# Layer B of a decoder trunk: splitting the next product's first weight piece inside the current product

## The chip, the core and the metric

The kernel runs on one core of a Trainium2 chip. The metric is the device time of one execution in microseconds, the median of several runs. The core's engines are named here as the profile names them: PE (TensorE, matmuls; PEld is its weight loads), DVE (VectorE), ACT (ScalarE), POOL (GpSimd) and SP (SyncE, which issues the DMAs of this kernel). TensorE's operands come from SBUF, and its sums go to PSUM.

## The reference, cut to what matters

A decoder trunk of two layers on 256 tokens of width 2048. Layer A is a Mamba-2 mixer. From its output come the keys and values that layer B, a dilated window attention with three head groups, uses. What layer B computes with large weights:

```python
k, v = jnp.split(x @ kv_w, 2, axis=-1)                 # kv_w: 2048 x 6144
shift, scale, gate = _adaln(c, ada_w[1], ada_b[1])     # silu(c) @ w + b, three columns of 2048
h = x * (1.0 + scale) + shift
q, z = jnp.split(h @ in_w, [DIL_Q_WIDTH], axis=-1)     # in_w: 2048 x 4096
o = ...                                                # attention of q over k, v, three groups merged
y = (o * jax.nn.silu(z)) @ out_w
x = _layer_norm(DEEPNORM_ALPHA * x + (1.0 + gate) * y, ln_g[1], ln_b[1])
```

All arrays are float32.

## The kernel before, in words

**Precision by splitting.** A float32 product is made of fp32r matmuls. Each operand is cut into a high half (a rounded copy) and a low half (the rest), and high x high, high x low and low x high are added up in PSUM. For weights this is `split` (L96): ScalarE copies `raw` to `whi` (L99), VectorE subtracts to `wlo` (L101). The activations of layer B stand ready split, as `xhi` and `xlo`, side by side in `xp`.

**Pieces and products.** Weights come in pieces of 128x1024 numbers, 512 KB each. `load_piece` (L91) has SP issue the DMA of one (L93) into one of six `raw` buffers; `whi` and `wlo` have four buffers each. A product runs over all 2048 rows of a weight block. `cm_wide` (L139) makes a block of 256 columns from four pieces; for each piece it runs eight matmuls of `whi` with both halves of the activations (L149, 512 columns) and eight of `wlo` with the high half (L152, 256 columns), in turns of two. `tm_chunk` (L181) makes a block of 512 columns from eight pieces (L173 to L175). The sums of a product take two of the four accumulators of the pool `mm`, so two products can be in PSUM at a time. Then they are emptied: after `cm_wide` by a copy on ScalarE (L156) and an addition on VectorE (L157) for each of two accumulators, after the value products by two copies on ScalarE in `evict_v` (L799).

**Layer B in order.** The value products of the first half (`wv`, the third of them by `tm_chunk`, L852), twelve key products by `cm_wide` (`wk`, L857), three more value products by `tm_chunk` (L859), the adaLN step on `xhi` and `xlo` (L863 to L868), six query products (`queries(0)`, L892 to L897), attention of the first four heads, six more query products, attention of the other four heads, four products of the gate path (`z_gate`), then the output product and the LayerNorm.

**The background.** `queue` (L267) makes a list of jobs, and `background` (L106) takes jobs from it at the end of each piece, at a rate that the product is given. In the key and value products the rate is one job for every two pieces. A job is a step of adaLN: it has SP load the next 128x2048 block of `ada_w` into one of two `araw` buffers (L244, 1 MB), and VectorE multiplies the block loaded before with silu(c) and adds up the products (L251). In the query products there is one job for every piece, sixteen in all (`weigh`, L878): products and sums on VectorE (L886), with two loads of rows (L63) in every fourth.

**What sets the order.** The program is traced once, and a planner sets the order of instructions on each engine: it plays the program through with its own costs, and gives an engine that is free the earliest traced of the instructions that are ready then. On the chip each engine, and SP's queue as well, runs its list in this fixed order and waits where it must. So the order on an engine is near the order of the trace, but an instruction that was ready later in the planner's play stands later. `tc.issue_after(ins)` queues what a block traces on the engine of `ins` behind `ins`; it orders the queue and does not wait for `ins` to end. The lists `copied` and `latest` hold the instructions of L99 and L101 as they are traced.

The order of the trace at the end of a product is now: load and split of the last piece, its matmuls, a background job if one is due, the two evictions, load and split of the next product's first piece, its matmuls.

Of the kernel before, what the change touches and what calls it, by code (L numbers as in the profile page):

```python
# [12 lines left out]
AF = mybir.ActivationFunctionType  # L13
ALU = mybir.AluOpType
# [7 lines left out]
KT = D // P  # L22
# [5 lines left out]
NG = 3  # L28
# [21 lines left out]
def trunk(ctx, tc, xT, x, c, par, cst, bias, lnrow, ada, wdt, win, wxs, wout, wk, wv, wbin, wbout, out):  # L50
    nc = tc.nc
    V, S, T, PO = nc.vector, nc.scalar, nc.tensor, nc.gpsimd
# [38 lines left out]
    def load_piece(src):  # L91
        raw = wp.tile([P, 1024], F32, name="raw", bufs=6)
        nc.sync.dma_start(raw, src)  # L93
        return raw

    def split(raw, into=None, after=None):  # L96

        hi, lo = into or [wp.tile([P, 1024], F32R, name=n, bufs=4) for n in ("whi", "wlo")]
        copied.append(S.activation(hi, raw, AF.Copy))  # L99
        with tc.issue_after(after) if after is not None else ExitStack():  # L100
            latest.append(V.tensor_tensor(lo, raw, hi.bitcast(F32), op=ALU.subtract))  # L101
        return hi.rearrange("p (k n) -> p k n", k=2), lo.rearrange("p (k n) -> p k n", k=2)

    jobs, latest, copied, pin = [], [], [], [None]

    def background(n, every=1):  # L106

# [7 lines left out]
    def cm_piece(src, q, ps, ahi, alo, k0=0, k1=KT, w=None, after=None):  # L115


        hi, lo = w or split(load_piece(src[q]), after=after)
        for k in range(2):
            kt = 2 * q + k  # L120
            for n in range(4):
                o = ps[n // 2][:, n % 2, :]
                c_ = slice(n * P, n * P + P)
                first = kt == k0 and n % 2 == 0
                T.matmul(o, hi[:, k, c_], ahi[:, kt, :], start=first, stop=False, skip_group_check=True)  # L125
                T.matmul(o, hi[:, k, c_], alo[:, kt, :], start=False, stop=False, skip_group_check=True)  # L126
                T.matmul(o, lo[:, k, c_], ahi[:, kt, :], start=False, stop=kt == k1 - 1, skip_group_check=True)  # L127
# [4 lines left out]
    def cm_quad(src, ahi, alo, rate=(0, 1), k0=0):  # L132
        ps = acc_pair()
        for q in range(k0 // 2, KT // 2):
            cm_piece(src, q, ps, ahi, alo, k0=k0)
            background(*rate)
        return ps

    def cm_wide(src, dst, rate=(0, 1), moving=None):  # L139

        both, high = moving or (lambda kt: xp[:, kt], lambda kt: xhi[:, kt, :])
        ps = acc_pair()
        for q in range(KT // 4):
            hi, lo = (t.rearrange("p k n -> p (k n)").rearrange("p (k n) -> p k n", k=4)
                      for t in split(load_piece(src[q])))
            for k in range(4):
                kt = 4 * q + k
                for n in range(2):
                    T.matmul(ps[n], hi[:, k, n * P:n * P + P], both(kt), start=kt == 0, stop=False,  # L149
                             skip_group_check=True)  # L150
                for n in range(2):
                    T.matmul(ps[n][:, 0, :], lo[:, k, n * P:n * P + P], high(kt), start=False, stop=kt == KT - 1,  # L152
                             skip_group_check=True)
            background(*rate)
        for n in range(2):
            S.activation(dst[:, n, :], ps[n][:, 1, :], AF.Copy)  # L156
            V.tensor_tensor(dst[:, n, :], ps[n][:, 0, :], dst[:, n, :], op=ALU.add)  # L157

    def tiles(ps):
        return [ps[n // 2][:, n % 2, :] for n in range(4)]  # L160
# [1 line left out]
    def tm_piece(src, q, ps, ahi, alo, k0=0, k1=KT, w=None):  # L162

        tm_mults(q, w or split(load_piece(src[q])), ps, ahi, alo, k0, k1, range(2))
# [16 lines left out]
    def tm_chunk(src, ahi, alo, nk=KT, rate=(0, 1), k0=0, pre=None, split_end=0):  # L181

        ps = tm_pair()
        n = nk // 2 - split_end
        for q in range(k0 // 2, n):
            if pre:
                pre(q)
            tm_piece(src, q, ps, ahi, alo, k0, nk)
            background(*rate)
        held = [(q, split(load_piece(src[q]))) for q in range(n, nk // 2)]  # L190
        for b in range(2):
            for q, w in held:
                tm_mults(q, w, ps, ahi, alo, k0, nk, (b,))
        return ps
# [63 lines left out]
    def gate_out(layer):  # L258

        ada_bias(layer, slice(0, KT), slice(2, 3))  # L260
        pt = aux.tile([P, 512], F32, name="aux")[:KT, :P]
        T.transpose(pt, mod[layer][:, :, 2], ident)
        row = sm.tile([KT, P], F32, name="row", bufs=1)
        V.tensor_copy(row, pt)
        nc.sync.dma_start(gated[layer].rearrange("(k p) -> k p", p=P), row)
# [24 lines left out]
    with ExitStack() as cA:  # L290
# [14 lines left out]
        with ExitStack() as cS:  # L305
# [75 lines left out]
            with ExitStack() as c0:  # L381
# [42 lines left out]
                for row in ("b4:0. b6:0. h z2:0. b2:0 x1:0 h", "b2:1. x1:1. z1:0 z1:1. z4:0 h h",  # L424
# [3 lines left out]
                    for w in row.split():  # L428
                        if w == two:
                            n = -2 if sum(o[0] == -2 for o in order) == sum(o[0] == -1 for o in order) else -1  # L430
# [359 lines left out]
    kv, vt = {}, {}  # L790
# [4 lines left out]

    def evict_v(hq, g, ps):
        vt[hq, g] = place(3 * hq + g if hq == 0 else 9 + g, [P, 2, 512])
        for b in range(2):
            S.activation(vt[hq, g][:, b, :], ps[b], AF.Copy)  # L799

    with ExitStack() as cL:
        pl = cL.enter_context(tc.tile_pool(name="pl", bufs=3))

        vps = [tm_pair(), tm_pair()]
        def high(i, b):
            for k in range(2):
                kt = 2 * (i // 2) + k
                for w in first_v[i]:
                    T.matmul(vps[i % 2][b], hx(kt)[:, b * P:b * P + P], w[:, k, :], start=kt == 0 and w is first_v[i][0],  # L809
                             stop=False)  # L810

        def low(i, b):
            for k in range(2):
                T.matmul(vps[i % 2][b], lx(2 * (i // 2) + k)[:, b * P:b * P + P], first_v[i][0][:, k, :], start=False,
                         stop=False)

        end, _ = x_quad(0)
        with tc.issue_after(end.ins):
            for n in range(1, 4):
                normalise(0, 512 * n, 512 * n + 512)  # L820
        for i in range(4):
            high(i, 0)
        for i in range(4):
            if i == 2:
                _, tile4 = x_quad(1)
                for n in range(1, 4):
                    normalise(1, 512 * n, 512 * n + 512)
            low(i, 0)
        for i in range(4):
            high(i, 1)  # L830
            if i == 2:
                x_tile(4)
                x_tile(5)
        for i in range(4):
            low(i, 1)
        for q in range(2, KT // 2):
            if q < KT // 2 - 1:
                x_tile(2 * q + 2)
                x_tile(2 * q + 3)
            for j in range(2):  # L840
                w = split(load_piece(wv[2 * j][q]), after=tile4.ins if q == 2 else None)
                tm_mults(q, w, vps[j], hx, lx, 0, KT, range(2))
        for g in range(2):
            evict_v(0, g, vps[g])

        R = (1, 2)
        pin[0] = latest[-1].ins
        with tc.issue_after(tile4.ins):
            state[0] = 0
            queue(pl, cols1[11:])  # L850
            jobs.append(lambda: gate_out(1))
            evict_v(0, 2, tm_chunk(wv[4], hx, lx, rate=R))  # L852
            for hq in range(2):
                for g in range(NG):
                    kv[hq, g] = place(3 + 3 * hq + g, [P, 4, L])
                    for w in range(2):
                        cm_wide(wk[2 * (2 * g + hq) + w], kv[hq, g][:, 2 * w:2 * w + 2, :], rate=R)  # L857
            for g in range(NG):
                evict_v(1, g, tm_chunk(wv[1 + 2 * g], hx, lx, rate=R))  # L859
            drain()  # L860
            late = latest[-1].ins

        ada_bias(1, slice(0, KT), slice(0, 2))  # L863
        for kt in range(KT):
            t = pl.tile([P, L], F32, name="htmp")
            S.activation(t, xhi[:, kt, :].bitcast(F32), AF.Identity, bias=shift(1, kt), scale=scale(1, kt))
            V.scalar_tensor_tensor(t, xlo[:, kt, :].bitcast(F32), scale(1, kt), t, op0=ALU.mult, op1=ALU.add)
            split_act(xhi[:, kt, :], xlo[:, kt, :], t)  # L868
# [22 lines left out]

    def queries(hq):  # L892
        qq = [pc2.tile([P, 4, L], F32, name=f"q{g}") for g in range(NG)]
        for g in range(NG):
            for w in range(2):
                cm_wide(wbin[2 * (2 * g + hq) + w], qq[g][:, 2 * w:2 * w + 2, :], rate=(1, 1))
        return qq  # L897
# [107 lines left out]
    ps = [tm_pair() for _ in range(2)]  # L1005
# [140 lines left out]
```

## Time and profile before

| | us |
|---|---|
| time, median of 3 runs | 1253.88 |
| lowest and highest of the runs | 1252.72, 1255.48 |
| the profiled execution's own time | 1253.52 |
| its span, first to last instruction | 1251.7 |
| PE busy | 1218.4 |
| weight loads of PE busy | 1043.1 |
| DVE busy | 1031.0 |
| ACT busy | 704.5 |

Everything that the profile shows belongs to the one profiled execution. A row of a timeline has the start in microseconds from the span's start, the duration (of all merged instructions), engine, line of the source, operation, what is written from what is read, the number of instructions merged (x2), and in brackets the idle time of the engine ahead of it and what ended that idle time. A row of the waits has who waited for whom: microseconds in total, times, the longest. A row of the busy time by stretch has the stretch, its length, busy time and number of instructions of PE, PEld, DVE, ACT and POOL, the granted clock of TensorE, the share of time that the DMA engines were busy, and GB/s. The ends of matmuls are modelled by the profiler.

The key, value and query products of layer B lie between about 750 and 1130 us of the span; the granted clock is 1.00 there.

### The profile page before, as it was taken

The numbers are of one execution on the slowest core, as the hardware profiler recorded it, in microseconds if no ns is written. First come the engines' busy times: TensorE is split into PE (matmuls) and PEld (weight loads), VectorE is DVE, ScalarE is ACT, GpSimd is POOL, SyncE is SP. The second block draws the span as 40 slices with busy tenths as digits, with TensorE's granted clock in tenths as the row PEclk, the third lists the DMA queues.
The fourth block names the chain that finished last, engine by engine and source line by source line (L and its number), as shares of the span: only waits on it lengthen the run. The fifth ranks groups of instructions, "written<-read, shape, count | busy, mean of one in ns | idle before, by whom it ended". The sixth has DMA issues, their size and how long they took to land.

```text
span 1251.7 us, 18740 instructions
## 1 busy us (share of the span) xinstructions
PE 1218.4 (97%) x7086; PEld 1043.1 (83%) x7086; DVE 1031.0 (82%) x1454; ACT 704.5 (56%) x1045; POOL 0.2 (0%) x4
## 2 busy tenths in 40 slices
PE   4999999999999999999999999999999999999997
PEld 4889998898888878788888788888878888888886
DVE  6999986999987988899778678879888866758777
ACT  3655477869588788754444544434445644445631
POOL 0000000000000000000000000000000000000000
PEclk9999999999999999999999999999999999999999
DMA  9999977687657556699998569989998774464641
GB/s 381 422 421 423 420 253 257 207 286 285 203 179 219 170 155 198 220 321 342 354 313 305 183 199 377 364 318 348 359 381 317 242 241 142 126 207 122 228 176 67
DMA packets 80586, 335.88 MB, mean 268 GB/s; under 512 B 9104, under 2 KB 9328, under 8 KB 67696
## 3 DMA queue, kind: packets, MB, share of 16 engines
q1 hardware_dynamic: 80496, 334.69, 74.7%
q8 instruction: 55, 0.90, 0.3%
q14 instruction: 35, 0.29, 0.1%
HBM read 332.47 MB, written 2.18 MB: 267 GB/s over the span
## 4 chain that ended last, share of the span: by engine, by line
PE 86%; DVE 6%; DMA 5%; issue 1%; ACT 1%; SPq 0%; DVEq 0%; ACTq 0%
PE acc L149 20%; PE acc L174 12%; PE acc L175 12%; PE acc L173 12%; PE acc L152 10%; PE acc L125 4%; PE acc L127 3%; PE acc L126 3%; DMA raw<-in_wk 3%; DMA araw<-in_ada 2%; DVE araw L251 1%; DVE wlo L101 1%; PE py L625 1%; DMA raw<-in_wv 1%; PE acc L809 1%
## 5 line engine op out<-in xcount | busy, mean ns | idle before, releaser
L99 ACT ACTIVATE whi<-raw 128x1024 fp32r<-128x1024 f32 x392 | 412.3, 1058 | 383.1 <-PE acc L175 142.1
L101 DVE TENSOR_TENSOR wlo<-raw,whi 128x1024 fp32r<-128x1024 f32 x392 | 473.5, 1222 | 141.0 <-ACT whi L99 137.0
L149 PE MATMUL acc<-actT,whi 128*128 128x512 f32 x1280 | 406.3, 398 | 0.0
L152 PEld LDWEIGHTS acc<-actT,wlo 128*128 128x128 f32 x1280 | 239.7, 188 | 62.2 <-DVE wlo L101 7.2
L174 PE MATMUL acc<-wlo,actT 128*128 128x512 f32 x688 | 269.9, 392 | 0.6 <-DVE wlo L101 0.5
L173 PE MATMUL acc<-whi,actT 128*128 128x512 f32 x688 | 266.6, 394 | 1.2 <-ACT actT L681 1.2
L152 PE MATMUL acc<-actT,wlo 128*128 128x256 f32 x1280 | 254.1, 280 | 3.9 <-DVE wlo L101 3.8
L251 DVE SCALAR_TENSOR_TENSOR araw<-araw,cb__72 128x2048 f32<-128x2048 f32 x96 | 219.4, 2285 | 8.9 <-DMA araw<-in_ada 8.6
L149 PEld LDWEIGHTS acc<-actT,whi 128*128 128x128 f32 x1280 | 196.5, 189 | 0.4
L175 PE MATMUL acc<-whi,actT 128*128 128x512 f32 x432 | 168.8, 391 | 0.0
L174 PEld LDWEIGHTS acc<-wlo,actT 128*128 128x128 f32 x688 | 129.3, 188 | 28.5 <-DVE wlo L101 2.8
L173 PEld LDWEIGHTS acc<-whi,actT 128*128 128x128 f32 x688 | 128.8, 188 | 27.2 <-ACT actT L681 1.7
L125 PE MATMUL acc<-actT,whi 128*128 128x256 f32 x384 | 109.0, 288 | 17.5 <-ACT actT L414 17.3
L126 PE MATMUL acc<-actT,whi 128*128 128x256 f32 x384 | 108.8, 286 | 0.0
L127 PE MATMUL acc<-actT,wlo 128*128 128x256 f32 x384 | 106.7, 286 | 1.9 <-DVE wlo L101 1.9
L175 PE MATMUL acc<-whi,ylo 128*128 128x512 f32 x256 | 100.7, 394 | 0.0
L175 PEld LDWEIGHTS acc<-whi,actT 128*128 128x128 f32 x432 | 81.1, 188 | 16.7
L125 PEld LDWEIGHTS acc<-actT,whi 128*128 128x128 f32 x384 | 74.3, 194 | 18.9 <-ACT actT L414 17.5
L127 PEld LDWEIGHTS acc<-actT,wlo 128*128 128x128 f32 x384 | 73.4, 195 | 2.2 <-DVE wlo L101 2.1
L126 PEld LDWEIGHTS acc<-actT,whi 128*128 128x128 f32 x384 | 74.7, 194 | 0.3
L175 PEld LDWEIGHTS acc<-whi,ylo 128*128 128x128 f32 x256 | 48.1, 188 | 9.7
L583 ACT ACTIVATE seg<-cbc,cumT 128x128 f32<-128x128 f32 x128 | 41.2, 390 | 5.6 <-PE py L625 4.9
(262 smaller groups left out, 1054.3 us busy)
## 6 DMA issues: line engine op xcount, KB each, us to landing
araw<-in_ada SPq DMA_DIRECT2D x96, 1024.0 KB, 7.7
raw<-in_win SPq DMA_DIRECT2D x112, 512.0 KB, 6.5
raw<-in_wout SPq DMA_DIRECT2D x64, 512.0 KB, 5.7
raw<-in_wbin SPq DMA_DIRECT2D x64, 512.0 KB, 4.1
raw<-in_wxs SPq DMA_DIRECT2D x48, 512.0 KB, 4.6
raw<-in_wv SPq DMA_DIRECT2D x48, 512.0 KB, 6.0
raw<-in_wk SPq DMA_DIRECT2D x48, 512.0 KB, 8.3
cbc<-cumd SPq DMA_DIRECT2D x16, 512.0 KB, 4.8
```

What stands on the lines that cost most here:

```text
L99: copied.append(S.activation(hi, raw, AF.Copy))
L101: latest.append(V.tensor_tensor(lo, raw, hi.bitcast(F32), op=ALU.subtract))
L125: T.matmul(o, hi[:, k, c_], ahi[:, kt, :], start=first, stop=False, skip_group_check=True)
L126: T.matmul(o, hi[:, k, c_], alo[:, kt, :], start=False, stop=False, skip_group_check=True)
L127: T.matmul(o, lo[:, k, c_], ahi[:, kt, :], start=False, stop=kt == k1 - 1, skip_group_check=True)
L149: T.matmul(ps[n], hi[:, k, n * P:n * P + P], both(kt), start=kt == 0, stop=False, skip_group_check=True)
L152: T.matmul(ps[n][:, 0, :], lo[:, k, n * P:n * P + P], high(kt), start=False, stop=kt == KT - 1, skip_group_check=True)
L173: T.matmul(o, h_, hi[:, k, :], start=kt == k0, stop=False, skip_group_check=part)
L174: T.matmul(o, h_, lo[:, k, :], start=False, stop=False, skip_group_check=part)
L175: end = T.matmul(o, l_, hi[:, k, :], start=False, stop=kt == k1 - 1, skip_group_check=part)
L251: V.scalar_tensor_tensor(raw, raw, 1.0, cb_, op0=ALU.mult, op1=ALU.mult, accum_out=mod[layer][:, ct, j:j + 1])
L583: S.activation(seg[:, hh, b, :], cbc[:, hh, b, :], AF.Relu, bias=cumT[:, b, h0 + hh:h0 + hh + 1], scale=-1.0)
```

## The change

The list `upcoming` names the products whose first piece is to be split early. When a product has split its own last piece and not yet traced its matmuls, `begin_next` loads and splits piece 0 of the next product in the list and keeps it in `ready`; the next product takes it from there (`first_or`). While `ready` holds a piece, `behind_next` queues the evictions on ScalarE behind the copy of that piece (`copied[-1]`) and those on VectorE behind its subtraction (`latest[-1]`).

The list is filled at two places. Ahead of the third value product: the twelve key products and the three value products that follow. In `queries`: the last five of its six query products. Elsewhere the list is empty, and then the order of the trace is as before. In a product that has a successor in the list, the order of the trace becomes: load and split of the last piece, load and split of the next product's first piece, the last piece's matmuls, a background job if one is due, the two evictions.

```diff
     jobs, latest, copied, pin = [], [], [], [None]
+    upcoming, ready = [], []
+
+    def first_or(src, q):
+
+        return ready.pop() if ready else split(load_piece(src[q]))
+
+    def begin_next():
+
+        if upcoming:
+            src, q = upcoming.pop(0)
+            ready.append(split(load_piece(src[q])))
+
+    def behind_next():
+
+        stack = ExitStack()
+        if ready:
+            stack.enter_context(tc.issue_after(copied[-1].ins))
+            stack.enter_context(tc.issue_after(latest[-1].ins))
+        return stack
...
     def cm_wide(src, dst, rate=(0, 1), moving=None):
...
         for q in range(KT // 4):
-            hi, lo = (t.rearrange("p k n -> p (k n)").rearrange("p (k n) -> p k n", k=4)
-                      for t in split(load_piece(src[q])))
+            w = first_or(src, q)
+            if q == KT // 4 - 1:
+                begin_next()
+            hi, lo = (t.rearrange("p k n -> p (k n)").rearrange("p (k n) -> p k n", k=4) for t in w)
...
-        for n in range(2):
-            S.activation(dst[:, n, :], ps[n][:, 1, :], AF.Copy)
-            V.tensor_tensor(dst[:, n, :], ps[n][:, 0, :], dst[:, n, :], op=ALU.add)
+        with behind_next():
+            for n in range(2):
+                S.activation(dst[:, n, :], ps[n][:, 1, :], AF.Copy)
+                V.tensor_tensor(dst[:, n, :], ps[n][:, 0, :], dst[:, n, :], op=ALU.add)
...
     def tm_chunk(src, ahi, alo, nk=KT, rate=(0, 1), k0=0, pre=None, split_end=0):
...
-            tm_piece(src, q, ps, ahi, alo, k0, nk)
+            w = first_or(src, q)
+            if q == nk // 2 - 1:
+                begin_next()
+            tm_piece(src, q, ps, ahi, alo, k0, nk, w=w)
...
     def evict_v(hq, g, ps):
...
-        for b in range(2):
-            S.activation(vt[hq, g][:, b, :], ps[b], AF.Copy)
+        with behind_next():
+            for b in range(2):
+                S.activation(vt[hq, g][:, b, :], ps[b], AF.Copy)
...
+            upcoming.extend((wk[2 * (2 * g + hq) + w], 0) for hq in range(2) for g in range(NG) for w in range(2))
+            upcoming.extend((wv[1 + 2 * g], 0) for g in range(NG))
             evict_v(0, 2, tm_chunk(wv[4], hx, lx, rate=R))
...
     def queries(hq):
         qq = [pc2.tile([P, 4, L], F32, name=f"q{g}") for g in range(NG)]
+        upcoming.extend([(wbin[2 * (2 * g + hq) + w], 0) for g in range(NG) for w in range(2)][1:])
```

`cm_quad`, which makes products of layer A, is changed in the same way as `tm_chunk`; the list is empty there.

More of the change, by code (lines that the diff above doesn't have):

```diff
@@ L134, in cm_quad @@
         for q in range(k0 // 2, KT // 2):
-            cm_piece(src, q, ps, ahi, alo, k0=k0)
+            w = first_or(src, q)
+            if q == KT // 2 - 1:
+                begin_next()
+            cm_piece(src, q, ps, ahi, alo, k0=k0, w=w)
             background(*rate)
@@ L187, in tm_chunk @@
                 pre(q)
-            tm_piece(src, q, ps, ahi, alo, k0, nk)
+            w = first_or(src, q)
+            if q == nk // 2 - 1:
+                begin_next()
+            tm_piece(src, q, ps, ahi, alo, k0, nk, w=w)
             background(*rate)
```

## The prediction

> **What bounds the kernel now.** I read the busy shares of the page first.
>
> ```profile
> span 1251.7 us, 18740 instructions
> ...
> PE 1218.4 (97%) x7086; PEld 1043.1 (83%) x7086; DVE 1031.0 (82%) x1454; ACT 704.5 (56%) x1045; POOL 0.2 (0%) x4
> ```
>
> TensorE is busy for 1218.4 of 1251.7 us. All its idle time is 33 us, and only the part that lies in layer B behind a product boundary can be what this change is after. The second view is the list of waits: a row of PE for the whole run, then rows for the stretch 840 to 960 us.
>
> ```profile
> PE acc L152 <- DVE wlo L101: 3.8, 7, 2.1
> ```
> ```profile
> PEld acc L152 <- DVE wlo L101: 4.3, 6, 1.4
> ...
> PEld acc L174 <- DVE wlo L101: 1.7, 4, 0.5
> PE acc L152 <- DVE wlo L101: 1.5, 5, 0.9
> ```
>
> In layer B, TensorE waits only for `wlo`, the low half of a weight piece, which VectorE makes (L101); it never waits for `whi`, nor for an accumulator. Because the ends of matmuls are modelled, I take the loss from boundaries and not from these gaps. The third view is busy time by stretch, cut where ScalarE begins to empty a key product (L156).
>
> ```profile
> 832.18:843.33 11.15, 11.15 (x66) 9.73 (x65) 8.59 (x9) 3.62 (x6) 0.00 (x0) 1.00 1.01 376
> 843.33:854.91 11.58, 11.43 (x66) 9.65 (x65) 9.81 (x10) 4.68 (x7) 0.00 (x0) 1.00 0.89 340
> ...
> 866.47:878.83 12.36, 11.42 (x66) 9.66 (x65) 11.00 (x13) 5.54 (x8) 0.00 (x0) 1.00 0.97 358
> ```
>
> The second number is the length. An undisturbed key product takes 11.15 us, so one of its four pieces takes 2.79. From 843.33 to 913.54 (both in ScalarE's rows below) lie six products: 70.21 us where 66.90 would do. They lose 3.31 us, once 1.2 and five times about 0.42. The value products behind lose in the same way: 4 waits of 1.7 us in the weight loads' rows, where the key products' 4.3 us of waits stand for 3.31 lost, so an estimated 1.7 x 3.31 / 4.3 = 1.3 us. Of the seven waits of PE in the run five lie in this stretch; one of the other two is in a query product, 0.4 more. **All that the change can win is 3.3 + 1.3 + 0.4 = 5.0 us.**
>
> **Where in a product the loss falls.** The product that begins at 854.82, on PE and then on VectorE:
>
> ```profile
> 854.82 0.62 PE L149 MATMUL acc<-actT,whi 128*128 128x512 f32 x2
> ...
> 861.18 0.50 PE L152 MATMUL acc<-actT,wlo 128*128 128x256 f32 x2 [0.15 <-DVE wlo L101]
> ```
> ```profile
> 850.60 2.29 DVE L251 SCALAR_TENSOR_TENSOR araw<-araw,cb__72 128x2048 f32<-128x2048 f32 x1
> ...
> 852.80 1.22 DVE L101 TENSOR_TENSOR wlo<-raw,whi 128x1024 fp32r<-128x1024 f32 x1
> 855.32 0.76 DVE L157 TENSOR_TENSOR s<-acc,s 128x256 f32<-128x256 f32 x2 [1.30 <-ACT s L156]
> 856.55 1.23 DVE L101 TENSOR_TENSOR wlo<-raw,whi 128x1024 fp32r<-128x1024 f32 x1 [0.47 <-ACT whi L99]
> 857.69 2.29 DVE L251 SCALAR_TENSOR_TENSOR araw<-araw,cb__72 128x2048 f32<-128x2048 f32 x1
> ...
> 859.90 2.36 DVE L101 TENSOR_TENSOR wlo<-raw,whi 128x1024 fp32r<-128x1024 f32 x2
> ```
>
> PE is held at 861.18, 6.36 us into the product, beyond two pieces of 2.79: at the **third** piece, not the first. VectorE's order there is: a dot product of the adaLN stage (L251), the low half of piece 0 (852.80, ahead of the boundary), the two additions that empty the accumulators (855.32), the low half of piece 1, another dot product of 2.29, the low halves of pieces 2 and 3. Piece 2's half runs from 859.90 for 1.22 until 861.12; PE wanted it at 854.82 + 5.58 + 0.47 = 860.87 (the 0.47 is two L149 matmuls, which need the high half alone). It is 0.25 late, and the restart of the matmuls makes that 0.42.
>
> **The change, part by part.** *1. The first piece is split a product early, and the evictions (L156 and L157, or L799) are queued behind it.* Which order stands now? ScalarE, around the last key product:
>
> ```profile
> 901.97 0.66 ACT L156 ACTIVATE b<-acc 128x256 f32<-128x256 f32 x2 [2.50 <-PE acc L152]
> 902.52 1.07 ACT L99 ACTIVATE whi<-raw 128x1024 fp32r<-128x1024 f32 x1
> 904.31 1.06 ACT L99 ACTIVATE whi<-raw 128x1024 fp32r<-128x1024 f32 x1 [0.72 <-DMA raw<-in_wk]
> 905.55 1.06 ACT L99 ACTIVATE whi<-raw 128x1024 fp32r<-128x1024 f32 x1 [0.18 <-DMA raw<-in_wk]
> 909.27 1.07 ACT L99 ACTIVATE whi<-raw 128x1024 fp32r<-128x1024 f32 x1 [2.65 <-DMA raw<-in_wv]
> 913.54 0.66 ACT L156 ACTIVATE b<-acc 128x256 f32<-128x256 f32 x2 [3.20 <-PE acc L152]
> ```
>
> The copy at 909.27 waits for `in_wv`: it is piece 0 of the value product that follows, and it stands ahead of the eviction of the last key product (913.54). Between two evictions lie four copies, as many as a product has pieces, so the eviction at 901.97 also stands behind piece 0 of its next product; counted back in the same way, so do all from 843.33 on. One boundary earlier the lead was two pieces, for between these evictions lie only three copies:
>
> ```profile
> 832.18 0.66 ACT L156 ACTIVATE s<-acc 128x256 f32<-128x256 f32 x2 [4.63 <-PE acc L152]
> 832.72 2.01 ACT L99 ACTIVATE whi<-raw 128x1024 fp32r<-128x1024 f32 x2
> 837.31 1.06 ACT L99 ACTIVATE whi<-raw 128x1024 fp32r<-128x1024 f32 x1 [2.58 <-DMA raw<-in_wk]
> 843.33 0.66 ACT L156 ACTIVATE s<-acc 128x256 f32<-128x256 f32 x2 [4.95 <-PE acc L152]
> ```
>
> VectorE has the same order: 852.80 before 855.32. In the query products the evictions stand further back still:
>
> ```profile
> 1036.38 1.06 ACT L99 ACTIVATE whi<-raw 128x1024 fp32r<-128x1024 f32 x1 [1.73 <-PE acc L149]
> 1037.34 0.64 ACT L156 ACTIVATE q<-acc 128x256 f32<-128x256 f32 x2
> ```
>
> The eviction has no wait in its row; the copy ahead of it waited for PE to give back a buffer. ScalarE is four `whi` buffers ahead there, so piece 3 of the next product stands before the eviction, and an earlier request would find no buffer. **At all 25 boundaries that the change names (12 key, 3 value, 10 query) the order that it asks for already stands, and this part is worth 0:** no eviction moves later, PE waits for no accumulator, and nothing new is held behind the evictions.
>
> The Trainium skill (Perfetto Trace Analysis, "Optimization Strategy") says that the same gap repeated over a stretch can mean too few buffers for the next tile; by it no order would help, and the 5.0 us would stay whatever is moved. The row of 1036.38 agrees for the query products, where hardly any time is lost; in the key products ScalarE's copies wait for data (0.72 and 0.18 above) and not for a buffer, so there the rows speak against it.
>
> *2. Piece 0's load and split move ahead of the background step behind the last piece.* That step is one load of `araw` (1 MB) and one dot product. SyncE's queue now:
>
> ```profile
> 848.43 0.33 SPq L244 DMA_DIRECT2D araw<-in_ada  x1
> 848.87 1.11 SPq L93 DMA_DIRECT2D raw<-in_wk  x2
> 852.92 0.33 SPq L244 DMA_DIRECT2D araw<-in_ada  x1
> 853.34 0.88 SPq L93 DMA_DIRECT2D raw<-in_wk  x2
> ```
>
> It is one `araw`, then two pieces, each time just as a dot product has ended (the one of 850.60 ends at 852.89 and gives back the buffer that the load of 852.92 takes): the pieces are held behind an `araw` load that waits. The pattern becomes one `araw` with three pieces, then one with one. Piece 0 is issued up to 4.5 us earlier (852.92 - 848.43); pieces 1 to 3 keep the same bytes ahead of them, since only piece 0 and one `araw` change places. VectorE takes its work in the order of landing, so the dot product and piece 0's half change places too: now dot from 850.60, half from 852.80, additions at 855.32; then half from 850.6, dot from 851.8 to 854.0, additions still at 855.3. The same work fits into the same hole, whose 1.30 us of idle time are the cover. Behind the boundary all stays: additions, piece 1, dot product, piece 2, and **the 0.42 us stay**, since they come from the dot product between pieces 1 and 2. If the cover goes, each further microsecond delays the additions and piece 1's half, which now ends at 857.78 where PE wants it at 854.82 + 2.79 + 0.47 = 858.08: 0.3 us of slack, then one for one.
>
> *3. Elsewhere.* Everything ahead of the last piece of the third value product keeps its order; there is nothing in the new list then. The query products keep theirs too. The one product that loses 1.2 (866.47 to 878.83) has three more VectorE operations than the others (x13, not x10); they may fall otherwise, between the usual 0.42 and 2.0: -0.8 to +0.8. The boundary at which the lead falls from two pieces to one may shift by one, 0.42 either way, and so may the query product's 0.4. Together -1.6 to +1.6; I take 0, as no row gives it a sign.
>
> **Sum.** 0 + 0 + 0 on the profiled execution's 1253.5 us (span 1251.7 and 1.8 around it): **1253.5 us**. The median of the runs is 1253.88, within 0.4 of it.
>
> **Rivals.** *A, faster.* The earlier load lets the planner put piece 1, too, ahead of the evictions, as at 832.18, where the product that follows loses nothing (11.15). For it: that lead of two did stand. Against: piece 1 remains behind the same `araw`. If it held at all later boundaries: 1253.5 - 5.0 = 1248.5; in the key products alone: 1253.5 - 3.3 = 1250.2. Chance 0.23.
>
> *B, slower.* The planner puts the dot product, which now lands later, between the additions and piece 1's half. Place: VectorE, just behind each boundary. Price: the additions end at 856.08, the dot product takes a net 2.2 (857.69 to 859.90), and the half ends 1.22 later, at 859.5, where PE wants it at 858.08: 1.4 late. The second dot product then makes piece 2 late by 0.3 more. That is 1.7 in place of 0.42, so 1.3 more for each boundary: over the nine from 843 us to the last value product 11.7, 1265.2; at half of them 1259.4. It decides as soon as the dot product's data land after PE has ended the product. Against it: they land when piece 0 lands today, and that is early enough today for piece 0's copy to stand before the eviction. For it: VectorE is the fullest helper (9.81 of 11.58 us), and with two `araw` buffers a load starts only when a dot product has ended. Chance 0.30.
>
> *C, the change does nothing of what it says,* the order being there already: that is my forecast itself. Chance 0.47, its own range 1251.9 to 1255.1 (part 3).
>
> **Range and chances.** A change under 0.2% (2.5 us) can't be told from none. Faster by more than that needs half of the 5.0 us back: 0.23. Slower by more needs rival B at two boundaries or more: 0.30. Within: 0.47. The range takes in most of A, and B at up to six or seven boundaries (6.5 x 1.3 = 8.5): 1249 to 1262.
>
> **What would show it.** Right: piece 0's copy ahead of each eviction, as before; SyncE's pattern turned into one `araw` with three pieces and one with one; key products still 11.57 us from eviction to eviction, with PE waiting for the third piece's `wlo`. Wrong on the fast side: two copies of the next product ahead of each eviction, and 11.15 throughout. Wrong on the slow side: L251 between L157 and the next L101 on VectorE and PE waiting at the second piece, or evictions so late that PE waits for an accumulator at L149, a wait that no row shows now. A product of layer B whose eviction stands today ahead of the next product's first copy would break the argument as a whole.

## The result, and the profile after

The changed kernel takes **1256.31 us**, the median of 20 runs (1252.37 to 1259.09), where the kernel before takes 1253.04 beside it, also of 20 runs (1251.38 to 1255.51). The ratio is 1.0024, with a 95% interval of 1.0016 to 1.0031: 3.3 us slower, a little more than the 0.2% up to which the forecast said "no change". The profiled execution of the changed kernel took 1252.37 us, the lowest of its 20 runs. Its trace therefore shows the order of the work, but hardly the loss; the traces of the experiments show that.

Line numbers of the changed kernel are higher: L149 and L152 (key and query matmuls) are now L173 and L176, L156 and L157 (evictions) L181 and L182, L173 to L175 (value matmuls) L198 to L200, L244 and L251 (`araw` load and dot product) L272 and L279, L886 (`weigh`) L917. L63, L93, L99 and L101 stay.

The head of the page:

```profile
span 1250.6 us, 18733 instructions
...
PE 1217.5 (97%) x7086; PEld 1042.7 (83%) x7086; DVE 1031.0 (82%) x1454; ACT 703.4 (56%) x1045; POOL 0.2 (0%) x4
```

**The key products.** Busy time by stretch, cut where ScalarE begins to empty a key product (columns as in the prediction):

```profile
830.51:841.66 11.15, 11.15 (x66) 9.73 (x65) 8.58 (x9) 3.62 (x6) 0.00 (x0) 1.00 0.98 380
841.66:853.22 11.56, 11.41 (x66) 9.64 (x65) 9.81 (x10) 4.45 (x6) 0.00 (x0) 1.00 0.82 323
...
864.79:877.26 12.47, 11.64 (x66) 9.72 (x65) 11.10 (x14) 6.05 (x10) 0.00 (x0) 1.00 0.92 363
...
sum 81.45, PE 79.87 PEld 67.69 DVE 68.74 ACT 32.60 POOL 0.00; mean PE 11.41 PEld 9.67 DVE 9.82 ACT 4.66 POOL 0.00
```

One product of 11.15 us, five of about 11.57 and one of 12.47: the picture of before, whose seven took 81.36 (832.18 to 913.54). ScalarE's timeline there, and then SyncE's queue:

```profile
841.66 0.66 ACT L181 ACTIVATE s<-acc 128x256 f32<-128x256 f32 x2 [7.41 <-PE acc L176]
842.20 3.90 ACT L99 ACTIVATE whi<-raw 128x1024 fp32r<-128x1024 f32 x4
853.22 0.66 ACT L181 ACTIVATE s<-acc 128x256 f32<-128x256 f32 x2 [7.12 <-PE acc L176]
```
```profile
833.92 0.33 SPq L272 DMA_DIRECT2D araw<-in_ada  x1
834.34 1.57 SPq L93 DMA_DIRECT2D raw<-in_wk  x3
839.54 0.33 SPq L272 DMA_DIRECT2D araw<-in_ada  x1
839.97 0.37 SPq L93 DMA_DIRECT2D raw<-in_wk  x1
```

Still four copies between two evictions, so each eviction stands behind one piece of the next product, as before. SyncE's pattern is the predicted one: an `araw` load with three pieces, then one with one. The pieces land earlier: ScalarE's waits for `raw` of `in_wk` between 750 and 1140 us are 1.1 us in all, 17.5 before. VectorE, around the boundary of 853.22:

```profile
846.66 3.49 DVE L101 TENSOR_TENSOR wlo<-raw,whi 128x1024 fp32r<-128x1024 f32 x3
850.06 2.29 DVE L279 SCALAR_TENSOR_TENSOR araw<-araw,cb__72 128x2048 f32<-128x2048 f32 x1
...
853.64 0.76 DVE L182 TENSOR_TENSOR s<-acc,s 128x256 f32<-128x256 f32 x2 [1.28 <-ACT s L181]
854.86 1.23 DVE L101 TENSOR_TENSOR wlo<-raw,whi 128x1024 fp32r<-128x1024 f32 x1 [0.47 <-ACT whi L99]
```

The dot product and piece 0's half (the last of the three at 846.66) have changed places, and 1.28 us of idle time stay in front of the additions, 1.30 before. TensorE's waits over the key and value products, then the first query eviction, of the kernel before and after:

```profile
PE acc L176 <- DVE wlo L101: 1.3, 4, 0.8
PE acc L199 <- DVE wlo L101: 0.6, 2, 0.3
```
```profile
992.33 0.64 ACT L156 ACTIVATE q<-acc 128x256 f32<-128x256 f32 x2
990.87 0.64 ACT L181 ACTIVATE q<-acc 128x256 f32<-128x256 f32 x2
```

The waits are 1.9 us, where before had 1.5, but the ends of matmuls are modelled, and the boundaries show less. From the key eviction with which the stretches begin to the first query eviction it is 160.36 us (990.87 - 830.51), where before had 160.15 (992.33 - 832.18): 0.2 more, and the same 160.36 in a second profiled execution of the changed kernel. So the loss of 3.3 us does not lie in the key and value products.

**The query products.** The next view is the timeline of VectorE, of the kernel before and then of the changed kernel in the second profiled execution (span 1255.9), in the third and fourth query products:

```profile
1004.36 1.29 DVE L886 TENSOR_TENSOR u<-u,pT 128x512 f32<-128x512 f32 x2 [2.77 <-DMA pT<-in_lnrow]
1006.04 0.69 DVE L886 TENSOR_TENSOR u<-u,pT 128x512 f32<-128x512 f32 x1 [0.39 <-DMA pT<-in_lnrow]
1006.65 1.22 DVE L101 TENSOR_TENSOR wlo<-raw,whi 128x1024 fp32r<-128x1024 f32 x1
1007.79 0.68 DVE L886 TENSOR_TENSOR u<-u,pT 128x512 f32<-128x512 f32 x1
```
```profile
1009.41 1.29 DVE L917 TENSOR_TENSOR u<-u,pT 128x512 f32<-128x512 f32 x2 [3.26 <-DMA pT<-in_lnrow]
1010.62 1.22 DVE L101 TENSOR_TENSOR wlo<-raw,whi 128x1024 fp32r<-128x1024 f32 x1
1011.76 0.69 DVE L917 TENSOR_TENSOR u<-u,pT 128x512 f32<-128x512 f32 x1
1012.36 1.22 DVE L101 TENSOR_TENSOR wlo<-raw,whi 128x1024 fp32r<-128x1024 f32 x1
1013.50 0.75 DVE L182 TENSOR_TENSOR q<-acc,q 128x256 f32<-128x256 f32 x2
1014.16 0.68 DVE L917 TENSOR_TENSOR u<-u,pT 128x512 f32<-128x512 f32 x1
...
1019.50 0.69 DVE L917 TENSOR_TENSOR u<-u,pT 128x512 f32<-128x512 f32 x1 [3.52 <-DMA pT<-in_lnrow]
1020.11 1.22 DVE L101 TENSOR_TENSOR wlo<-raw,whi 128x1024 fp32r<-128x1024 f32 x1
```

`weigh` takes four operations for each pair of row loads (`lnrow` into the one tile `pT`), and the next pair cannot be loaded until the fourth has ended. Before, one weight half stands among the four of the third pair, and the fourth begins 3.43 us after the first (1007.79 - 1004.36). After, two halves and the evictions stand among them: 4.75 us (1014.16 - 1009.41). SyncE issues the fourth pair when that operation has ended, before at 1008.50 and after at 1014.87. VectorE has come to the pair's first operation 3.52 us before the rows land, and waits; the weight half that TensorE needs next stands behind. TensorE of that execution:

```profile
1011.90 0.51 PE L176 MATMUL acc<-actT,wlo 128*128 128x256 f32 x2 [0.91 <-DVE wlo L101]
...
1021.38 0.50 PE L176 MATMUL acc<-actT,wlo 128*128 128x256 f32 x2 [0.85 <-DVE wlo L101]
```

Both waits end with the half that came just behind a row wait (1010.62 and 1020.11, 1.22 each).

### The profile page after: what moved, and what is told of

It is laid out like the page before. It is cut to its first block, busy times and chain, and to the rows that moved or that the text cites. A ratio compares the mean times of both kernels' runs of the same rounds, so it can differ in the third digit from the quotient of the medians.

```text
span 1250.6 us, 18733 instructions
## 1 busy us (share of the span) xinstructions
PE 1217.5 (97%) x7086; PEld 1042.7 (83%) x7086; DVE 1031.0 (82%) x1454; ACT 703.4 (56%) x1045; POOL 0.2 (0%) x4
## 4 chain that ended last, share of the span: by engine, by line
PE 84%; DVE 7%; DMA 5%; ACT 2%; issue 2%; SPq 0%; DVEq 0%; ACTq 0%
PE acc L173 20%; PE acc L199 12%; PE acc L200 12%; PE acc L198 12%; PE acc L176 10%; PE acc L144 3%; PE acc L146 3%; PE acc L145 3%; DVE wlo L101 2%; DMA araw<-in_ada 2%; PE py L653 1%; DVE araw L279 1%; ACT whi L99 1%; DMA raw<-in_wk 1%; DMA raw<-in_wv 1%
## 5 line engine op out<-in xcount | busy, mean ns | idle before, releaser
L99 ACT ACTIVATE whi<-raw 128x1024 fp32r<-128x1024 f32 x392 | 411.3, 1059 | 355.7 <-PE acc L200 148.9
L101 DVE TENSOR_TENSOR wlo<-raw,whi 128x1024 fp32r<-128x1024 f32 x392 | 473.4, 1222 | 144.4 <-ACT whi L99 140.2
L173 PE MATMUL acc<-actT,whi 128*128 128x512 f32 x1280 | 405.2, 397 | 0.0
L176 PEld LDWEIGHTS acc<-actT,wlo 128*128 128x128 f32 x1280 | 238.9, 188 | 62.1 <-DVE wlo L101 7.4
L198 PE MATMUL acc<-whi,actT 128*128 128x512 f32 x688 | 266.6, 394 | 1.2 <-ACT actT L709 1.2
L176 PE MATMUL acc<-actT,wlo 128*128 128x256 f32 x1280 | 253.7, 279 | 3.8 <-DVE wlo L101 3.4
L279 DVE SCALAR_TENSOR_TENSOR araw<-araw,cb__72 128x2048 f32<-128x2048 f32 x96 | 219.4, 2286 | 10.4 <-DMA araw<-in_ada 10.1
L173 PEld LDWEIGHTS acc<-actT,whi 128*128 128x128 f32 x1280 | 195.8, 189 | 0.5
L200 PE MATMUL acc<-whi,actT 128*128 128x512 f32 x432 | 168.8, 391 | 0.0
L198 PEld LDWEIGHTS acc<-whi,actT 128*128 128x128 f32 x688 | 128.9, 188 | 27.1 <-ACT actT L709 1.7
L144 PE MATMUL acc<-actT,whi 128*128 128x256 f32 x384 | 109.0, 288 | 17.5 <-ACT actT L442 17.4
L200 PE MATMUL acc<-whi,ylo 128*128 128x512 f32 x256 | 100.7, 394 | 0.0
L200 PEld LDWEIGHTS acc<-whi,actT 128*128 128x128 f32 x432 | 81.1, 188 | 16.7
L200 PEld LDWEIGHTS acc<-whi,ylo 128*128 128x128 f32 x256 | 48.1, 188 | 9.7
```

The source lines that it names most:

```text
L198: T.matmul(o, h_, hi[:, k, :], start=kt == k0, stop=False, skip_group_check=part)
L200: end = T.matmul(o, l_, hi[:, k, :], start=False, stop=kt == k1 - 1, skip_group_check=part)
L279: V.scalar_tensor_tensor(raw, raw, 1.0, cb_, op0=ALU.mult, op1=ALU.mult, accum_out=mod[layer][:, ct, j:j + 1])
```

## The experiments

Three theories stood. **Theory 1:** the new load order costs time in the key and value products. **Theory 2:** the query products lose it, because VectorE stands at the rows of `weigh` with weight halves behind. **Theory 3:** nothing in layer B; executions differ.

**The changed kernel again**, and **only the load early** (the split stays where it was, no evictions queued). The order of the latter is that of the changed kernel, but that on VectorE one `weigh` operation and the weight half ahead of it change places:

```diff
-        return ready.pop() if ready else split(load_piece(src[q]))
+        return split(ready.pop() if ready else load_piece(src[q]))
...
-            ready.append(split(load_piece(src[q])))
+            ready.append(load_piece(src[q]))
...
-            stack.enter_context(tc.issue_after(copied[-1].ins))
-            stack.enter_context(tc.issue_after(latest[-1].ins))
+            pass
```

> The changed kernel once more, for the trace of a typical execution (the one that was profiled, 1252.37 us, was the fastest of twenty, whose median is 1256.31). Theory 1 (the new order of loads in the key and value products loses time in executions whose transfers land late): 2 to 4 us over the kernel before, and a trace over 1255 us shows new waits between 770 and 960 us, behind late landings of araw or raw. Theory 2 (the query products lose it, where a weight piece now goes ahead of two loads of lnrow): 2 to 4 us, new waits between 985 and 1030 us. Theory 3 (nothing in layer B, a spread between executions and chips): within 1 us of the kernel before on the same chip.

> Only the load of the next product's first piece moves into the current product; its split stays where it was, and nothing is queued behind it. Theory 1: all of the loss, 2 to 4 us, since it is the queue of loads that matters. If the moved split or the queueing of the evictions were the cause: within 1 us of the kernel before. Theory 3: within 1 us.

Measured: 1256.94 us, ratio 1.0024 (1.0013 to 1.0035), and 1255.26, ratio 1.0017 (1.0006 to 1.0029), beside 1253.68 for the kernel before. The early load alone has most of the effect or all of it. The queueing by `issue_after` adds none: with and without it the planner gives every engine the same order.

**One half of the list each**, twice:

```diff
-        upcoming.extend([(wbin[2 * (2 * g + hq) + w], 0) for g in range(NG) for w in range(2)][1:])
```
```diff
-            upcoming.extend((wk[2 * (2 * g + hq) + w], 0) for hq in range(2) for g in range(NG) for w in range(2))
-            upcoming.extend((wv[1 + 2 * g], 0) for g in range(NG))
```

> The change at the key and value products alone; the query products as before. Theory 1: all of the loss, 2 to 4 us. Theory 2: within 1 us of the kernel before. Theory 3: within 1 us.

> The early piece in key and value products alone, a second sample (the first: ratio 1.0009, interval 0.9997 to 1.0021). Theory 2 in its simple form (the early piece of the query products does it): ratio 1.000. If the part in the key and value products, by the place at which it leaves DVE when the queries begin, does it: 1.001 to 1.002.

> The change at the query products alone; the key and value products as before. Theory 1: within 1 us of the kernel before. Theory 2: 2 to 4 us slower. Theory 3: within 1 us.

> The early piece in query products alone, a second sample (the first: ratio 1.0011, interval 0.9998 to 1.0023). Theory 2 in its simple form: 1.002 to 1.0025, all of the change. If both parts have a share: 1.001.

Key and value products alone: 1254.28, ratio 1.0009 (0.9997 to 1.0021), then 1256.73, ratio 1.0020 (1.0009 to 1.0031). Query products alone: 1253.99, ratio 1.0011 (0.9998 to 1.0023), then 1254.26, ratio 1.0003 (0.9991 to 1.0015). The simple form of theory 2, that the early piece of the query products does it, falls: the part in the key and value products weighs at least as much. Yet its traces show the loss in the query products, whose order on VectorE it changes too.

**How late rows become lost time.** Eight traces, of five kernels, have the same `weigh` and differ in the order around it or in the execution. In each I took the third and the fourth eviction of a query product on ScalarE (an undisturbed product takes 11.15 us), and the start of the `weigh` operation just ahead of the half that TensorE needs then. From timelines of all engines, in this order: the key and value part alone (second run), only the load early, the query part alone (second run), the kernel before:

```profile
1015.73 0.64 ACT L181 ACTIVATE q<-acc 128x256 f32<-128x256 f32 x2
...
1017.19 0.69 DVE L917 TENSOR_TENSOR u<-u,pT 128x512 f32<-128x512 f32 x1 [3.92 <-DMA pT<-in_lnrow]
...
1028.01 0.64 ACT L181 ACTIVATE q<-acc 128x256 f32<-128x256 f32 x2
```
```profile
1013.19 0.64 ACT L180 ACTIVATE q<-acc 128x256 f32<-128x256 f32 x2
...
1015.06 0.69 DVE L916 TENSOR_TENSOR u<-u,pT 128x512 f32<-128x512 f32 x1 [4.22 <-DMA pT<-in_lnrow]
...
1025.88 0.64 ACT L180 ACTIVATE q<-acc 128x256 f32<-128x256 f32 x2
```
```profile
1012.48 0.69 DVE L915 TENSOR_TENSOR u<-u,pT 128x512 f32<-128x512 f32 x1 [3.18 <-DMA pT<-in_lnrow]
...
1012.49 0.64 ACT L181 ACTIVATE q<-acc 128x256 f32<-128x256 f32 x2
...
1023.64 0.64 ACT L181 ACTIVATE q<-acc 128x256 f32<-128x256 f32 x2
```
```profile
1012.55 1.29 DVE L886 TENSOR_TENSOR u<-u,pT 128x512 f32<-128x512 f32 x2 [1.14 <-DMA pT<-in_lnrow]
...
1014.62 0.64 ACT L156 ACTIVATE q<-acc 128x256 f32<-128x256 f32 x2
...
1015.37 0.69 DVE L886 TENSOR_TENSOR u<-u,pT 128x512 f32<-128x512 f32 x1 [1.52 <-DMA pT<-in_lnrow]
...
1026.20 0.64 ACT L156 ACTIVATE q<-acc 128x256 f32<-128x256 f32 x2
```

| trace | fourth pair issued ahead of the third eviction | `weigh` starts after it | product longer than 11.15 by |
|---|---|---|---|
| before | 6.12 | 0.75 (second row) | 0.43 |
| queries alone, first and second run | 4.43, 4.30 | 0.43, -0.01 | 0.13, 0.00 |
| after | 3.45 | 0.73 | 0.42 |
| keys and values alone, first and second run | 3.70, 3.57 | 1.15, 1.46 | 0.82, 1.13 |
| after, second execution | 3.18 | 1.45 | 1.12 |
| only the load early | 3.46 | 1.87 | 1.54 |

In all eight the loss is the third column less 0.32 (0 where that is negative), to 0.02 us. The second column is what the order sets: before, the pair is issued 6.1 us ahead, in the full change and its key and value part 3.2 to 3.7, in the query part alone 4.3 to 4.4. The first row of the pair took 4.03 to 5.31 us to land. So with a lead of 3.2 to 3.7 all five executions lost something, with 4.3 to 4.4 only the one whose row came later did, and with 6.1 the first row cost nothing. That fits both: each part has a share, and executions of one kernel differ in these products.

**The rows left out** of both kernels, with the sixteen operations of `weigh` (the output then lacks that scaling):

```diff
-    jobs.extend(lambda n=n, b=b, i=i: weigh(n, b, i) for n in range(4) for i in range(2) for b in range(2))
```

> The kernel before with the sixteen multiplications and additions of the normalisation's rows into u (weigh) and their eight row loads left out, so the output lacks that scaling; nothing else moves on PE or ACT. It serves as the base for the next run. Theory 2 (the query products lose time behind the row loads): 1252.5 to 1253.5, since the kernel before loses at most about 0.3 us there; the PE waits for wlo between 965 and 1060 us are gone. Theory 1 (the loss sits in the key and value products): 1253 to 1254. Theory 3 (spread): the same as the kernel before.

> The changed kernel with the same sixteen operations and eight row loads left out (output lacks that scaling). Theory 2: within 1 us of the run above (only the key stage's 0.2 us stays), so about 1253, and 2 to 3 us under the changed kernel. Theory 1: still 2 to 3 us above the run above, about 1256. Theory 3 (differences between executions outside layer B): 2 to 3 us above, with no stage of layer B that shows them.

Measured beside 1253.64 for the kernel before: 1253.22, ratio 0.9996 (0.9986 to 1.0005), and 1253.58, ratio 1.0002 (0.9994 to 1.0011). Without the rows the change costs 0.4 us by the medians, too little to be told from nothing here; the 0.2 us of the key and value products would fit in it. Theories 1 and 3 fall. But these runs leave out VectorE's work together with the loads, so they do not say which of the two it is.

**The rows kept, in two buffers.** All of VectorE's work stays, and every second pair of rows goes into the score tiles, which are free then:

```diff
-            t = pc2.tile([P, 1024], F32, name="pT", bufs=1)
-            lnr[n] = [t[:, 512 * j:512 * j + 512] for j in range(2)]
+            if n % 2:
+                lnr[n] = [pc2.tile([P, 512], F32, name=f"sc{j}", bufs=1) for j in range(2)]
+            else:
+                t = pc2.tile([P, 1024], F32, name="pT", bufs=1)
+                lnr[n] = [t[:, 512 * j:512 * j + 512] for j in range(2)]
```

> The changed kernel, where the second and fourth pair of row loads go into the two score tiles in place of the one row tile, so that a pair can be loaded while the pair before is still in use. Theory 2: the rows land before DVE comes to them, the loss of 0.2 to 1.9 us in the query products goes, 1253 to 1254.5. Theory 1 and 3: 1256, as the changed kernel.

> The kernel before with the second and fourth row pair in the score tiles: the control for the same edit of the changed kernel, which gave 1253.25. Theory 2 (the rows cost the changed kernel 2 to 3 us and the one before at most 0.4): 1253 to 1253.7, the same as the kernel before, so that with this edit the two orders are equal. Theory 1: 1250 to 1251, 2 to 3 us under the changed kernel with this edit.

The changed kernel with it: 1253.25, ratio 0.9993 (0.9985 to 1.0002) to the kernel before. The kernel before with it: 1253.55, ratio 0.9998 (0.9987 to 1.0008). The edit does nothing for the kernel before and takes back the whole loss of the changed one. VectorE's waits for rows between 983 and 1060 us, in the changed kernel with the edit:

```profile
DVE u L920 <- DMA pT<-in_lnrow: 1.1, 2, 0.8
...
DVE u L920 <- DMA sc<-in_lnrow: 0.9, 1, 0.9
```

Two us in place of 11.3 in the second execution of the changed kernel, and TensorE has no wait in that stretch.

**What the change could have won.** The prediction put the 0.42 us of a key product down to the dot product between pieces 1 and 2. So from the third value product on every piece, not only the first of a product, is loaded and split one piece ahead of the background step. What is shown here of the products is `cm_wide`; `tm_chunk` gets the same two lines, and `ahead[0]` becomes true where the first list is filled. Then the same with the row edit above:

```diff
-    upcoming, ready = [], []
+    upcoming, ready, ahead = [], [], [False]
...
             if q == KT // 4 - 1:
                 begin_next()
+            elif ahead[0]:
+                ready.append(split(load_piece(src[q + 1])))
...
+            ahead[0] = True
```

> The changed kernel, where from the last value product of the first half on every weight piece (not only the first of a product) is loaded and split one piece ahead of the background step. If the 0.42 us per key product go with the dot product that stands before the third piece's half, and if query products no longer wait behind the rows: 1253 minus 2.5 to 5, 1248 to 1250.5. If the second dot product only moves to another piece: 1253 to 1256.

> Halves one piece ahead, and the second and fourth row pair in the score tiles. Halves ahead gave 1249.4, with 0.42 us left in the key stage and 0.86 us in the query stage of its trace. If the rows cost it there too: 1247.5 to 1248.5, with no wait for wlo between 965 and 1060 us. If it does not stand in the way any more: 1249 to 1250.

Measured: **1249.39**, ratio 0.9967 (0.9956 to 0.9979), and **1248.31**, ratio 0.9955 (0.9940 to 0.9970), both below the kernel before (1253.6 beside them) and the changed one. The first still has 0.9 us of waits for `wlo` in the query products, the second none. Of the second, the stretches between key evictions, VectorE in one of them, and all of TensorE's waits over key and value products:

```profile
842.74:853.89 11.15, 11.15 (x66) 9.73 (x65) 9.81 (x10) 4.45 (x6) 0.00 (x0) 1.00 0.88 335
...
sum 78.08, PE 78.08 PEld 68.02 DVE 68.72 ACT 32.59 POOL 0.00; mean PE 11.15 PEld 9.72 DVE 9.82 ACT 4.66 POOL 0.00
```
```profile
843.16 0.76 DVE L184 TENSOR_TENSOR s<-acc,s 128x256 f32<-128x256 f32 x2 [2.01 <-ACT s L183]
844.38 2.36 DVE L101 TENSOR_TENSOR wlo<-raw,whi 128x1024 fp32r<-128x1024 f32 x2 [0.47 <-ACT whi L99]
846.66 2.28 DVE L283 SCALAR_TENSOR_TENSOR araw<-araw,cb__72 128x2048 f32<-128x2048 f32 x1
```
```profile
PE acc L201 <- DVE wlo L101: 0.4, 1, 0.4
```

Two halves now stand ahead of the dot product behind a boundary, with the same ten VectorE operations and 9.81 us of work in the product. Seven key products take 78.08 us, where the kernel before took 81.36: 3.3 us, of 5.3 by which this kernel is faster than that one.

## Why the prediction was wrong

**What bounds the kernel** was right: five waits of the third piece, 0.42 each, and about 5.0 us to be won. The last experiment won 5.3. That the two agree so well is in part luck: in its trace the key products gave the 3.3 us that were counted and the query products the 0.4, but the value products, up to the first query eviction, only 0.5 of the estimated 1.3 (78.33 us, 78.79 before). The remaining 1.1 us were timed, but do not lie in these products of the trace.

**Part 1, the order that the change asks for stands already: right.** Four copies between evictions, as before, and `issue_after` alters no engine's order.

**Part 2, the load moves, the swap hides, the 0.42 us stay: right.** SyncE's pattern, the 1.28 us of cover and the seven key products (81.45 us, 81.36 before) came as said. The 0.2 us more up to the first query eviction lie inside the 1.6 of part 3.

**Part 3 is the step that failed:** "The query products keep theirs too", with 0 taken, "as no row gives it a sign". The change measured 3.3 us slower, more than that part's own 1.6, and with a second row buffer nothing of the loss was left. The query evictions do keep their place, but the order has more in it: VectorE's `weigh` operations and weight halves fall otherwise, and the next row loads wait for `weigh`. The rows that give the sign were in the trace of before: waits of 2.77, 1.14 and 1.52 us for `pT` on VectorE, with weight halves behind them and the 0.43 us of the table as the first loss. The prediction counted one query loss of 0.4 and did not ask what made it. It asked of SyncE's queue only what `araw` and the pieces do, and not what the row loads wait for.

**Rival A** did not come: from 841.66 us on no second piece stands ahead of an eviction. **Rival B** had the sign and, in kind, the mechanism (a background operation on VectorE ahead of a half that TensorE needs), but at another place: no dot product (L279) stands between the additions and the next half from 841.66 us on, and the cost in the traces is not 1.3 us per boundary but 0 to 2.3 us in all, in the third and fourth query products. The range up to 1262 was there for rival B at its own place, so it is luck that 1256.31 lies within it.

The rule of the Trainium skill that the prediction weighed (Perfetto Trace Analysis, "Optimization Strategy": a gap that repeats can mean too few buffers) can now be set against runs. In the key products too few buffers were not the reason: order alone, with the same buffers, took the repeated 0.42 away. For the rows they were: a second buffer took the loss away.

**What stays open.** In the five traces with the lead of 3.2 to 3.7 us, the stretch from the first to the fourth query eviction is 0.4 to 2.3 us longer than the undisturbed 33.44 (mean 1.2; before 0.4). The difference of 0.8 and the 0.2 of the key and value products make about 1.0 us, while the medians of the runs to which these traces belong were 0.6 to 3.3 us above the kernel before (mean 2.4; 3.3 for the full change). The runs without rows and with two row buffers bind nearly all of the timed loss to the row waits; why the medians show more than these five executions lost was not settled.

## What to carry to other kernels

When a change moves one instruction in a planned order, follow the background work through the next stage too: on an in-order engine an operation that waits for a load holds everything behind it, and if the load's only buffer is given back by an operation in the same queue, each instruction put among them delays the next load. Before moving an eviction or a load, see which piece the tensor engine is late for; here it was the third, and splitting every piece one step ahead of the background, with a second row buffer, gave the 5 us that an early first piece could not.

## What the runs showed of the hardware

A load of one row to all partitions (256 KB written) took 3.0 to 8.0 us from issue to landing in the two traces of the changed kernel, while the median of a 512 KB piece of the query weights, in the same queue, was 4.2 and 4.0 us: the smaller load did not land sooner. And the time of one kernel spread over 6.7 us in 20 runs, though the granted clock of every profiled execution was 0.997 to 1.000. A trace of one execution, here the fastest, can miss the stall that sets the median.

Much of the difference between traces arises ahead of the stages that the change touches. The first value product is emptied at 749.74 us in one trace of the changed kernel and at 753.45 in the other: 3.7 of the 5.3 us between their spans, where the query products account for 1.9. Over all fourteen traces that moment lies between 749.30 and 754.08, although up to it every engine's order is the same in all of them. One part of it is a wait of TensorE for VectorE's `ylo` in layer A, between 500 and 590 us: 1.3 to 2.3 us in five traces, of both orders, and 0.3 to 0.4 in the other nine.
